# A down product from split operands, and a new order of the arms in an expert loop

## The chip, the cores and the metric

The kernel runs on one core of a Trainium2 chip. The metric is the time of one execution in device microseconds. The core's engines run side by side and meet at semaphores: TensorE (PE in the profile; PEld is its weight load), VectorE (DVE), ScalarE (ACT), GpSimd (POOL) and SyncE (SP). Each has a sequencer that reads its own instruction stream, takes the branches in it and hands the rest to the engine. A row with a q behind the engine (PEldq) is of the sequencer: a branch, a register load or a wait.

## The reference, cut to what matters

Two layers over 1024 latent and 256 context tokens of width 1024. Each ends in a mixture of experts: every token is given to two of 32 experts, and each expert computes

```
def expert_block(args):
    tb, e = args
    xb = h[tb]
    return (jax.nn.silu(xb @ wg[e]) * (xb @ wu[e])) @ wd[e]
```

with `wg`, `wu` of 1024 x 512 and `wd`, the down weights, of 512 x 1024, all float32. The results are scaled by the gates and added up per token. Layer 0 routes all 1280 tokens, layer 1 the 1024 latent ones. How many tokens an expert gets is known only when the router has run.

## The kernel before

After the attention of a layer, `moe` runs the 32 experts one after the other, in straight code with one copy per place `e` in the loop. Experts 0 and 1 always have places 0 and 1 (`FIX`); the others are sorted by size, largest first, when the router is done. `n` is the number of chunks of 64 tokens that the expert at a place has; each engine loads it into a register and branches on it.

The arms differ in `n`. With n=1, `half` multiplies 64 tokens in float32. With n=2, `full` multiplies 128 tokens by gate and up weights together: operands are split into a high and a low part in the type FP32R (`split`: ScalarE copies, VectorE subtracts), and three products of the parts (`mm3`) take the place of one in float32. With n=3 a `full` and a `half` follow each other (`large`). With n=4 `double` computes 256 tokens, and above that `more` takes the rest in pieces. The down product (`down`) is in float32 in every arm: for up to 128 tokens eight matmuls, from four slices `g[:, k]` of the hidden values and two halves of the output.

A place in the loop runs so: first product, then the activation (`act`, ScalarE and VectorE), its transposes (`ht`) mixed with those of the next expert's input (`xt_pe`), the down product, `prep` for the next expert (three of its eight weight slices and its input are split ahead, where its n is over 1), `evac` from PSUM, and the scatter of the rows. The eight weight slices pass through four pairs of buffers, `WS[0]` to `WS[3]`, so slice k uses the pair k % 4. Weights arrive by SyncE's queue in a ring of 14 units, six to an expert, and a unit is loaded again when its last reader is done.

For the order of the code: `with tc.If(...)` lays out the block under it and then the one under `Else`; an engine jumps past the block that it doesn't take. In the first half of the loop (`e < NE // 2`) the long arm stands first:

```
with tc.If(n > 2, preferred_fallthrough_block=True) as c:
    large(e, n, ps, p2, y2, g2)
    nc.tensor.addr_align(256, offset=0, max_nops=0)
with c.Else():
    with tc.If(n > 1, preferred_fallthrough_block=True) as c2:
        full(ps, e)
```

In the second half `half` stands first, then `large`, then `full`. Inside `large` the test L2296 (n < 4) stands ahead of the block for n=3, L2300 (n > 4) ahead of that for n over 4, and the block for n=4 comes last. The lines that the text speaks of: L2345 is the test n > 2 ahead of the first product in the first half of the loop, L2347 the alignment at the long arm's end, L2377 the test n > 2 ahead of the down product; L2115 is the matmul of `half`, L175 to L177 are those of `mm3`, L2082 the transposes of the next input, L2181 the down product, L170 and L171 the two steps of `split`, L2164 VectorE's part of the activation, L2186 and L2187 the evacuation.

Of the kernel before, what the change touches and what calls it, by code (L numbers as in the profile page):

```python
# [10 lines left out]
F32R = mybir.dt.float32r  # L11
# [11 lines left out]
NE = 32  # L23
# [121 lines left out]
class Kernel:  # L145
# [1905 lines left out]
    def moe(self):  # L2051
# [3 lines left out]
        with ExitStack() as ctx:  # L2055
# [8 lines left out]
            self.ring += [wp.tile([128, 2048], F32, name=f"es{i}") for i in range(NU - NU0)]  # L2064
            WS = [(wp.tile([128, 1024], F32R, name=f"wh{i}"), wp.tile([128, 1024], F32R, name=f"wl{i}")) for i in range(NS)]
            G = [sp.tile([128, 4, 128], F32, name=f"g{i}") for i in range(2)]
            SG = [sp.tile([128, 256], F32, name=f"sg{i}") for i in range(2)]
            iv = sp.tile([128, 3], I32, name="iv")
            XT = [sp.tile([128, KD, 128], F32, name=f"xT{i}") for i in range(2)]
# [20 lines left out]
            def xt(x, n):  # L2090
                xt_copy(xt_pe(x), n)
# [16 lines left out]
            def half(ps, e):  # L2108


                x = XT[e % 2]
                for k in range(KD):
                    w = self.unit(e, k // 2)[:, k % 2]
                    for o in range(2):
                        nc.tensor.matmul(ps[0][64 * o:64 * o + 64, :], x[:, k, 0:64], w[:, :, o * 256:(o + 1) * 256],  # L2115
                                         start=(k == 0), stop=(k == KD - 1))
# [8 lines left out]
            def prod(ps, i, k, ns=NS, os=range(2)):  # L2125
                h, lo = [w.rearrange("p (s n) -> p s n", s=2) for w in WS[k % ns]]
                for o in os:
                    c = slice(o * 256, o * 256 + 256)
                    self.mm3(ps[o], XS[i][0][:, k, :], XS[i][1][:, k, :], h[:, :, c], lo[:, :, c],
                             k == 0, k == KD - 1)  # L2130

            def full(ps, e, x=None):

                for k in range(KD - 2):
                    if k + AHEAD < KD:
                        ws(e, k + AHEAD)
                    prod(ps, 0, k)
                for o in range(2):
                    for k in range(KD - 2, KD):
                        prod(ps, 0, k, NS, (o,))  # L2140
                    if x is not None and o == 0:
                        xt(x, e)

            def double(ps, p2, e, m):

# [119 lines left out]
            N = {}  # L2265

            def load_n(e):
                N[e] = nc.values_load(self.seq[0:1, 0, e:e + 1], min_val=0, max_val=2 * nt)
                if e >= FIX:
                    self.E[e] = nc.values_load(self.seq[0:1, 1, e:e + 1], engines=LOADS, min_val=0, max_val=NE - 1)  # L2270

# [21 lines left out]

            def large(e, n, ps, p2, y2, g2):

                with tc.If(n < 4) as c3:  # L2296
                    full(ps, e, xg[2 + e % 3])
                    half(p2, e)
                with c3.Else():
                    with tc.If(n > 4) as c4:  # L2300
                        double(ps, p2, e, 5)
                        hidden(p2, g2)
                        down(g2, e, False)
                        evac(y2)
                        scatter(y2, places(e, 1))
                        more(e, n, 2, p2, g2)
                    with c4.Else():
                        double(ps, p2, e, 4)

            def large_down(e, n, p2, y2, g, g2, pl):  # L2310
                down(g, e, False, (0,))
# [23 lines left out]
            for e in range(NE):  # L2335
                n = N.pop(e)
                nxt = e + 1 if e + 1 < NE else None
                if e + 3 < NE:
                    load_n(e + 3)
                if e + 2 < NE:  # L2340
                    gather(xg[e % 2], first(e + 2, 0, "a"))
                ps, p2, y, y2, g, g2 = GU[e % 2], GU[1 - e % 2], Y[e % 2], Y[1 - e % 2], G[e % 2], G[1 - e % 2]
                if e < NE // 2:

                    with tc.If(n > 2, preferred_fallthrough_block=True) as c:  # L2345
                        large(e, n, ps, p2, y2, g2)
                        nc.tensor.addr_align(256, offset=0, max_nops=0)  # L2347
                    with c.Else():
                        with tc.If(n > 1, preferred_fallthrough_block=True) as c2:
                            full(ps, e)  # L2350
                        with c2.Else():
                            half(ps, e)
                else:
                    with tc.If(n < 2) as c:
                        half(ps, e)
                    with c.Else():
                        with tc.If(n > 2) as c2:
                            large(e, n, ps, p2, y2, g2)
                        with c2.Else():
                            full(ps, e)  # L2360
                self.e_loads(e * 6 + 4 + NU)
                pl = sp.tile([128, 2], I32, name="pl", bufs=4)
                for o, z in enumerate((self.idx_v, self.idx_w)):
                    nc.vector.tensor_copy(pl[:, o:o + 1], z[:, 0, at(e)])
                if e + 3 < NE:
                    over(e + 3)
                s0, s1 = act(ps, 0), act(ps, 1)
                if nxt:
                    x = xt_pe(xg[nxt % 2], (0,))
                ht(ps, s0, g, 0)  # L2370
                if nxt:
                    x += xt_pe(xg[nxt % 2], (1,))
                ht(ps, s1, g, 1)
                if nxt:
                    xt_copy(x, nxt)
                if e < NE // 2:
                    with tc.If(n > 2, preferred_fallthrough_block=True) as c:  # L2377
                        large_down(e, n, p2, y2, g, g2, pl)
                    with c.Else():
                        with tc.If(n > 1, preferred_fallthrough_block=True) as c2:  # L2380
                            down(g, e, False)
                        with c2.Else():
                            down(g, e, True)
                else:
                    with tc.If(n < 2) as c:
                        down(g, e, True)
                    with c.Else():
                        with tc.If(n > 2) as c2:
                            large_down(e, n, p2, y2, g, g2, pl)
                        with c2.Else():  # L2390
                            down(g, e, False)
                if nxt:
                    with tc.If(N[nxt] > 1):
                        prep(nxt)
                evac(y)
                self.e_loads(e * 6 + 6 + NU)
                scatter(y, [pl[:, o:o + 1] for o in range(2)])
                if e >= NE - 3:
                    self.marks.append(nc.gpsimd.memset(self.spacer, 0.0))
                if e == 2:  # L2400
                    self.route_gates()
# [147 lines left out]
```

## Time and profile before

| | |
|---|---|
| Median of three runs | 3205.91 us (3199.2 to 3206.66) |
| The profiled execution | 3205.89 us, of which the span is 3204.1 us |
| TensorE busy | 2653.9 us, 83% of the span |
| VectorE, ScalarE busy | 1507.2 us (47%), 1187.7 us (37%) |
| DMA moved | 617.02 MB, mean 193 GB/s |

The span goes from the first instruction to the last. Busy time counts instructions of the engine itself, not its sequencer's. The expert loop of layer 0 runs from about 868 to 1645 us, that of layer 1 from about 2382 to 3140 us. One float32 matmul gives two records of TensorE, one in FP32R a single record.

### The profile page before, as it was taken

What the parts mean: (1) busy time and instruction counts of PE and PEld (TensorE: products, weight loads), DVE (VectorE), ACT (ScalarE), POOL (GpSimd) and SP (SyncE); (2) the same over time, 40 slices, a digit from 0 to 9 for tenths busy, and PEclk for the clock granted to TensorE, in tenths of its full rate; (3) what the DMA queues carried; (4) which work ended last, traced back from release to release, by engine and by line L of the source; (5) the groups of instructions that cost most, each with busy time, mean ns of one, the idle gap of its engine ahead of it and who ended that gap; (6) DMA issues with size and microseconds to landing.
All of it is one profiled execution on the core that took longest, in us unless ns stands there. A gap on an engine that the chain in (4) does not pass through costs nothing. (4 is left out here: it accounts for less than half of the span.)

```text
span 3204.1 us, 43663 instructions
## 1 busy us (share of the span) xinstructions
PE 2653.9 (83%) x13122; PEld 1670.8 (52%) x13122; DVE 1507.2 (47%) x2981; ACT 1187.7 (37%) x2260; POOL 1064.8 (33%) x919
## 2 busy tenths in 40 slices
PE   6988899998489888987748989999848888887873
PEld 3766556576356445543317765566634455632321
DVE  3355556477644345521149555556852335511115
ACT  3223766632043334511135337665202335511112
POOL 1023999223311121111236349941331111112214
PEclk8988999999699999999978999999969999999987
DMA  7542000042665558899985530002274457799995
GB/s 268 216 139 81 1 1 1 1 157 79 236 245 189 198 181 307 311 351 361 349 315 186 185 136 1 1 1 99 86 260 167 158 196 267 294 363 369 354 357 238
DMA packets 280646, 617.02 MB, mean 193 GB/s; under 512 B 63376, under 2 KB 77072, under 8 KB 271504
## 3 DMA queue, kind: packets, MB, share of 16 engines
q1 hardware_dynamic: 253872, 566.43, 49.0%
q0 software_dynamic: 24544, 37.91, 3.4%
q8 instruction: 281, 4.60, 0.6%
q10 hardware_dynamic: 1536, 4.69, 0.4%
q14 instruction: 413, 3.38, 0.3%
HBM read 577.09 MB, written 73.81 MB: 203 GB/s over the span
## 5 line engine op out<-in xcount | busy, mean ns | idle before, releaser
L2195 POOL DMA_INDIRECT y_d<-my,pl x150 | 166.1, 1107 | 451.2 <-ACT wh L170 194.5
L1330 DVE TENSOR_REDUCE mx<-S 128x1 f32<-128x1024 f32 (+1 forms) x272 | 215.3, 799 | 210.7 <-PE S L1325 210.4
L2181 PE MATMUL mpy<-er,g 128*64 128x512 f32 (+1 forms) x656 | 239.7, 665 | 6.9 <-issue 6.7
L2194 POOL MEMSET spacer<- 128x1 f32 x152 | 17.5, 115 | 665.9 <-DMA y_d<-my,pl 520.5
L175 PE MATMUL gu<-wh,xh 128*128 128x512 f32 x432 | 183.2, 424 | 47.1 <-issue 12.6
L2082 PE MATMUL mtp<-ident,xg 128*128 128x128 f32 x600 | 107.2, 314 | 138.9 <-issue 85.6
L2163 ACT ACTIVATE sg<-gu 128x256 f32<-128x256 f32 x152 | 50.3, 383 | 461.3 <-PE gu L2115 313.9
L1342 ACT ACTIVATE P<-S,nb 128x256 f32<-128x256 f32 (+1 forms) x272 | 208.3, 772 | 33.5 <-DVE nb L1334 32.2
L1356 ACT ACTIVATE PT<-pt 128x512 f32<-128x512 f32 (+1 forms) x321 | 169.1, 531 | 138.2 <-PE pt L1347 129.5
L1347 PE MATMUL pt<-ident,P 128*128 128x128 f32 x1312 | 207.2, 283 | 11.3 <-ACT P L1342 11.1
L2164 DVE TENSOR_TENSOR sg<-gu,sg 128x256 f32<-128x256 f32 x152 | 57.7, 420 | 334.9 <-ACT sg L2163 308.1
L1391 PE MATMUL po<-PT,V 128*64 128x256 f32 x1312 | 215.0, 408 | 0.1
L181 POOL TENSOR_TENSOR rs_out<-ln_ve,mhalf 128x1 f32<-128x1 f32 x64 | 58.7, 917 | 451.0 <-DVE ln_ve L200 292.6
L1347 PEld LDWEIGHTS pt<-ident,P 128*128 128x128 f32 x1312 | 145.2, 141 | 85.5 <-ACT P L1342 42.2
L176 PE MATMUL gu<-wl,xh 128*128 128x512 f32 x432 | 179.5, 416 | 8.9 <-DVE wl L171 8.8
L177 PE MATMUL gu<-wh,xl 128*128 128x512 f32 x432 | 177.4, 411 | 0.0
L2082 PEld LDWEIGHTS mtp<-ident,xg 128*128 128x128 f32 x600 | 82.6, 162 | 178.2 <-issue 167.1
L2115 PE MATMUL gu<-er,xT 128*64 128x512 f32 x704 | 162.2, 607 | 12.3 <-DMA er<-in_w_e_gate 4.8
L1324 PE MATMUL S<-KH,Q 128*128 128x512 f32 (+1 forms) x400 | 168.3, 422 | 1.6 <-ACT P L1342 1.6
L2187 DVE COPY my<-mpy 128x512 f32<-128x512 f32 x75 | 51.7, 690 | 233.9 <-PE mpy L2181 217.6
L171 DVE TENSOR_TENSOR wl<-er,wh 128x1024 fp32r<-128x1024 f32 x106 | 128.1, 1222 | 70.6 <-ACT wh L170 62.7
L1222 POOL TENSOR_TENSOR Y<-Y 128x1310 f32<-128x1310 f32 (+1 forms) x60 | 150.6, 2510 | 5.0
(407 smaller groups left out, 6350.4 us busy)
## 6 DMA issues: line engine op xcount, KB each, us to landing
er<-in_w_e_down SPq DMA_DIRECT2D x66, 1024.0 KB
er<-in_w_e_gate SPq DMA_DIRECT2D x130, 512.0 KB
er<-in_w_e_up SPq DMA_DIRECT2D x130, 512.0 KB
raw<-in_w_mod SPq DMA_DIRECT2D x40, 1024.0 KB
es<-in_w_e_gate SPq DMA_DIRECT2D x68, 512.0 KB
es<-in_w_e_up SPq DMA_DIRECT2D x68, 512.0 KB
es<-in_w_e_down SPq DMA_DIRECT2D x32, 1024.0 KB
raw<-in_w_e_gate SPq DMA_DIRECT2D x40, 512.0 KB
```

The lines of the kernel that those rows point to most:

```text
L175: t.matmul(ps, lh, rh, start=start, stop=False)
L176: t.matmul(ps, lh, rl, start=False, stop=False)
L177: t.matmul(ps, ll, rh, start=False, stop=stop)
L1324: tens.matmul(x[:, c:c + w], q, self.KH[:, g, o:o + w], start=True, stop=False)
L1330: v.tensor_reduce(S[st, "mx"][:, ci:ci + 1], S[st, ci][:, 0:cs[ci][1]], axis=AX.X, op=OP.max)
L1342: act.activation(P[st][:, c:c + w], S[st, ci][:, :w], AF.Exp, bias=S[st, "nb"], accum_out=SU[pi][:, i, h, ci:ci + 1])
L1347: tens.transpose(tp[:, j, :], P[st][:, (g_ * 4 + j) * 128:(g_ * 4 + j + 1) * 128], self.ident)
L1356: act.activation(d, TP[st, g_][:, :m, :], AF.Copy)
L1391: tens.matmul(PO[key][o * 64:o * 64 + 64, :], self.V[:, k0(pi) + j, hp // 2, :], PT[pi, 2 * hp + o][:, j, :], start=(j == 0), stop=(j == n ...
L2082: nc.tensor.transpose(tp[:, j, :], x[:, k * 128:(k + 1) * 128], self.ident)
L2181: nc.tensor.matmul(py[o][64 * o:64 * o + 64, :] if hf else py[o], g[:, k % 2, z:z + 64] if hf else g[:, k, :], self.unit(e, 4 + k // 2)[:, ...
L2195: s = nc.gpsimd.indirect_dma_start(out=self.y_d[0:2 * T, :].rearrange("t (h d) -> (t h) d", h=2), out_offset=bass.IndirectOffsetOnAxis(ap= ...
```

## The change

There is a new down product, `down3`, for n=2. Slice 0 of the hidden values stays in float32. Slices 1 to 3 are split into new tiles `GS`, and the down weights of these slices are split too (`wd`), into the pairs `WS[1]` to `WS[3]`; each then goes through `mm3`. The weights of slice 1 are split near the end of `full` (`dn=True`), those of slices 2 and 3 inside `down3`, when the pairs' last weights of the first product have been read.

In `large` the tests are now n > 3 and, in it, n > 4; the block for n=3 comes last. Experts 0 and 1 take the layout of the second half, with `half` first, and their n is read from `nch` in place of `seq`, the same numbers.

```
@@ def full
-            def full(ps, e, x=None):
+            def full(ps, e, x=None, dn=False):
...
                         ws(e, k + AHEAD)
                     prod(ps, 0, k)
+                if dn:
+                    wd(e, 1)
                 for o in range(2):
                     for k in range(KD - 2, KD):
                         prod(ps, 0, k, NS, (o,))
...
+            def wd(e, k):
+                self.split(*WS[k], self.unit(e, 4 + k // 2)[:, k % 2])
+
+            def down3(g, e):
+                gh, gl = GS
+                for o in range(2):
+                    nc.tensor.matmul(py[o], g[:, 0, :], self.unit(e, 4)[:, 0, o * 512:o * 512 + 512], start=True, stop=False)
+                self.split(gh, gl, g[:, 1:4, :])
+                for k in range(1, 4):
+                    if k > 1:
+                        wd(e, k)
+                    h, lo = WS[k]
+                    for o in range(2):
+                        c = slice(o * 512, o * 512 + 512)
+                        self.mm3(py[o], gh[:, k - 1, :], gl[:, k - 1, :], h[:, c], lo[:, c], False, k == 3)
@@ def load_n
-                N[e] = nc.values_load(self.seq[0:1, 0, e:e + 1], min_val=0, max_val=2 * nt)
+                row = self.nch[0:1, 0, e:e + 1] if e < FIX else self.seq[0:1, 0, e:e + 1]
+                N[e] = nc.values_load(row, min_val=0, max_val=2 * nt)
@@ def large
-                with tc.If(n < 4) as c3:
-                    full(ps, e, xg[2 + e % 3])
-                    half(p2, e)
-                with c3.Else():
-                    with tc.If(n > 4) as c4:
+                with tc.If(n > 3, preferred_fallthrough_block=True) as c3:
+                    with tc.If(n > 4, preferred_fallthrough_block=True) as c4:
                         double(ps, p2, e, 5)
...
                     with c4.Else():
                         double(ps, p2, e, 4)
+                with c3.Else():
+                    full(ps, e, xg[2 + e % 3])
+                    half(p2, e)
@@ the loop over experts, first product
-                if e < NE // 2:
+                if FIX <= e < NE // 2:
...
-                            full(ps, e)
+                            full(ps, e, dn=True)
@@ the loop over experts, down product
-                if e < NE // 2:
+                if FIX <= e < NE // 2:
...
-                            down(g, e, False)
+                            down3(g, e)
```

On TensorE the arm for n=2 of the down product, from its test (L2380 before, L2403 now) to the test ahead of the next expert's first product (L2345 before, L2368 now). `mpy` is the PSUM pair, `er` a ring unit, `g` the hidden values, `gs` their split, `wh` and `wl` the pairs of WS. Before:

```order
L2380 COMPARE_AND_BRANCH
L2181 MATMUL mpy_7378<-er_7087,g_7393 128x512 [waits DMAHW1_49,Activation_49]
L2181 MATMUL mpy_7378<-er_7087,g_7393 128x512
L2181 MATMUL mpy_7378<-er_7088,g_7393 128x512 [waits DMAHW3_49,DMAHW2_49,Activation_49]
L2181 MATMUL mpy_7378<-er_7088,g_7393 128x512
...
L2181 MATMUL mpy_7379<-er_7088,g_7393 128x512 [waits DMAHW4_49]
...
L2345 COMPARE_AND_BRANCH
```

Now:

```order
L2403 COMPARE_AND_BRANCH
L2156 MATMUL mpy_7378<-er_7085,g_7393 128x512 [waits DMAHW5_49,Activation_49]
L2156 MATMUL mpy_7379<-er_7085,g_7393 128x512 [waits DMAHW6_49]
L175 MATMUL mpy_7378<-wh_7386,gs_7394 128x512 [waits Activation_49]
...
L177 MATMUL mpy_7378<-wh_7386,gs_7395 128x512 [waits DVE_49]
...
L175 MATMUL mpy_7378<-wh_7390,gs_7394 128x512 [waits Activation_49]
L176 MATMUL mpy_7378<-wl_7391,gs_7394 128x512 [waits DVE_49]
...
L2368 COMPARE_AND_BRANCH
```

The last wait ahead of the next test was one for a DMA in the seventh of eight matmuls; now it is one for VectorE's low part of slice 3, five records from the end.

On VectorE between the same two places; `xl` is the low part of the next expert's input. Before:

```order
L2380 COMPARE_AND_BRANCH
L2393 COMPARE_AND_BRANCH
L171 TENSOR_TENSOR wl_7385<-er_7089,wh_7384 128x1024 [waits DMAHW4_49,DMAHW3_49,DMAHW5_49,DVE_49,Activation_49]
L171 TENSOR_TENSOR xl<-xT_7397,xh 128x512 [waits Activation_49]
L171 TENSOR_TENSOR wl_7387<-er_7089,wh_7386 128x1024 [waits DVE_49,Activation_49]
```

Now:

```order
L2403 COMPARE_AND_BRANCH
L171 TENSOR_TENSOR gs_7395<-g_7393,gs_7394 128x384 [waits DVE_49,Activation_49]
L171 TENSOR_TENSOR wl_7389<-er_7086,wh_7388 128x1024 [waits DMAHW6_49,DMAHW0_49,DMAHW7_49,DVE_49,Activation_49]
L171 TENSOR_TENSOR wl_7391<-er_7086,wh_7390 128x1024 [waits DVE_49,Activation_49]
...
L2416 COMPARE_AND_BRANCH
L171 TENSOR_TENSOR wl_7385<-er_7087,wh_7384 128x1024 [waits DMAHW1_49,DMAHW0_49,DMAHW7_49,DVE_49,Activation_49]
L171 TENSOR_TENSOR xl<-xT_7399,xh 128x512 [waits Activation_49]
```

Three subtractions stand ahead of `prep`'s five; ScalarE has the three copies for them at the same place.

On TensorE the start of the loop in layer 0, as a piece of the difference; `gu` is the PSUM pair of the first product.

```order
-L2268 TENSOR_LOAD seq
-L2345 COMPARE_AND_BRANCH
-L2296 COMPARE_AND_BRANCH
...
+L2291 TENSOR_LOAD seq
+L2377 COMPARE_AND_BRANCH
+L2116 MATMUL gu_7374<-raw,xT_7399 64x512 x8
...
+L2377 UNCONDITIONAL_BRANCH
+L2380 COMPARE_AND_BRANCH
+L2319 COMPARE_AND_BRANCH
+L2320 COMPARE_AND_BRANCH
```

Behind the first test now stands the half product, and then the tests of the long arm, L2319 (n > 3) and L2320 (n > 4); before, the long arm came behind it.

## Rows read from the trace of the kernel before

**Rows 1.** Page, part 1: the span

```profile
span 3204.1 us, 43663 instructions
```

**Rows 2.** N=2 stretches: span, busy PE PEld DVE ACT POOL, clock, DMA, GB/s

```profile
1172.00:1386.00 214.00, 191.81 (x696) 125.34 (x692) 116.80 (x153) 101.71 (x140) 34.46 (x49) 0.96 0.81 297
...
2652.00:2818.00 166.00, 147.21 (x540) 96.41 (x539) 89.95 (x120) 78.56 (x108) 27.78 (x42) 0.97 0.82 298
```

**Rows 3.** Timeline, ScalarE's evacuations at n=2: start, length, instruction [idle <-releaser]

```profile
1200.66 0.60 ACT L2186 ACTIVATE my<-mpy 128x512 f32<-128x512 f32 x1 [0.85 <-ACT wh L170]
...
1245.82 0.60 ACT L2186 ACTIVATE my<-mpy 128x512 f32<-128x512 f32 x1 [0.86 <-ACT wh L170]
...
1267.35 0.60 ACT L2186 ACTIVATE my<-mpy 128x512 f32<-128x512 f32 x1 [0.84 <-ACT wh L170]
...
1361.00 0.60 ACT L2186 ACTIVATE my<-mpy 128x512 f32<-128x512 f32 x1 [0.84 <-ACT wh L170]
```

**Rows 4.** Timeline of one seam at n=2, all engines

```profile
1238.02 0.76 DVE L2164 TENSOR_TENSOR sg<-gu,sg 128x256 f32<-128x256 f32 x2 [3.59 <-ACT sg L2163]
...
1239.49 1.95 PE L2181 MATMUL mpy<-er,g 128*128 128x512 f32 x4
...
1240.97 1.06 ACT L170 ACTIVATE wh<-es 128x1024 fp32r<-128x1024 f32 x1 [0.47 <-ACTq L2377]
...
1244.72 1.88 PE L2181 MATMUL mpy<-ox,g 128*128 128x512 f32 x4
...
1247.63 0.47 PE L175 MATMUL gu<-wh,xh 128*128 128x512 f32 x1 [1.03 <-DVE my L2187]
...
1247.94 0.40 PE L176 MATMUL gu<-wl,xh 128*128 128x512 f32 x1
...
1248.18 0.40 PE L177 MATMUL gu<-wh,xl 128*128 128x512 f32 x1
```

**Rows 5.** TensorE's sequencer: ns (min/median/max), first and last start

```profile
L2377 PEldq COMPARE_BRANCH  x1: 362/362/362, 1238.8 to 1238.8; - x1
...
L2345 PEldq COMPARE_BRANCH  x1: 6183/6183/6183, 1241.1 to 1241.1; - x1
...
L2345 PEldq COMPARE_BRANCH  x7: 6039/6078/6183, 1196.0 to 1330.8; - x7
...
L2345 PEldq COMPARE_BRANCH  x1: 6687/6687/6687, 868.7 to 868.7; - x1
...
L2345 PEldq COMPARE_BRANCH  x1: 4416/4416/4416, 2650.7 to 2650.7; - x1
```

**Rows 6.** Timeline of TensorE before the first half product of layer 0

```profile
875.92 1.12 PE L2115 MATMUL gu<-raw,xT 128*64 128x512 f32 x2 [7.73 <-ACTq L2349]
```

**Rows 7.** Lines, steps of a split: count, busy us, mean ns, idle

```profile
L170 ACT ACTIVATE wh<-er 128x1024 fp32r<-128x1024 f32 x106 | 111.2, 1055 | 69.0 <-PE gu L177 29.5 <-issue 20.5 <-DVE wl L171 3.3
...
L171 DVE TENSOR_TENSOR wl<-er,wh 128x1024 fp32r<-128x1024 f32 x106 | 128.1, 1222 | 70.6 <-ACT wh L170 62.7
```

**Rows 8.** Stretches around a gap of TensorE, columns as in group 2

```profile
917.00:922.90 5.90, 0.00 (x0) 0.00 (x0) 0.45 (x2) 0.00 (x0) 2.85 (x4) 0.88 1.04 367
...
922.90:928.00 5.10, 5.04 (x16) 4.29 (x17) 0.21 (x1) 1.07 (x2) 0.00 (x0) 0.50 0.79 305
...
928.00:947.00 19.00, 18.24 (x78) 14.44 (x78) 8.08 (x11) 6.09 (x7) 0.67 (x1) 0.99 0.01 3
```

**Rows 9.** TensorE at the end of n=3 (and of n=4, third row)

```profile
1075.49 0.87 PE L2082 MATMUL mtp<-ident,xg 128*128 128x128 f32 x3 [7.40 <-issue]
...
L2347 PEldq COMPARE_BRANCH  x1: 6289/6289/6289, 1068.4 to 1068.4; - x1
...
L2347 PEldq COMPARE_BRANCH  x1: 291/291/291, 945.7 to 945.7; - x1
```

**Rows 10.** Timeline of TensorE in layer 1: first matmuls of places 0 to 3

```profile
2390.38 1.12 PE L2115 MATMUL gu<-raw,xT 128*64 128x512 f32 x2 [7.79 <-ACTq L2349]
...
2410.71 1.98 PE L2115 MATMUL gu<-er,xT 128*64 128x512 f32 x4 [4.77 <-DMA er<-in_w_e_gate]
...
2428.72 0.47 PE L175 MATMUL gu<-wh,xh 128*128 128x512 f32 x1 [2.37 <-ACT my L2186]
...
2523.48 0.76 PE L175 MATMUL gu<-wh,xh 128*128 128x512 f32 x1 [5.76 <-issue]
```

More of the change, by code (lines that the diff above doesn't have):

```diff
@@ L2066, in moe @@
             G = [sp.tile([128, 4, 128], F32, name=f"g{i}") for i in range(2)]
+            GS = [sp.tile([128, 3, 128], F32R, name=f"gs{i}") for i in range(2)]
             SG = [sp.tile([128, 256], F32, name=f"sg{i}") for i in range(2)]
@@ L2359, in moe @@
                         with c2.Else():
-                            full(ps, e)
+                            full(ps, e, dn=True)
                 self.e_loads(e * 6 + 4 + NU)
@@ L2390, in moe @@
                         with c2.Else():
-                            down(g, e, False)
+                            down3(g, e)
                 if nxt:
```

## The prediction

> **What bounds the kernel now.** I read the page's first part, then the stretches of the two expert loops, then TensorE's rows and its sequencer's within single stages. The span is 3204.1 us [rows 1]; the change touches only the two expert loops. The reference's router, run on its inputs, gives how many half chunks n (of 64 tokens) each expert has, and so which arm runs where. Layer 0: expert 0 has n=1, expert 1 n=2, then three with n=4, three with n=3, nine with n=2, fifteen with n=1. Layer 1: experts 0 and 1 n=1, then 7, 4, 4, 3, seven with n=2, nineteen with n=1. So 17 of 64 experts take the new down product, and 16 of them stand in the first half of the loop, where the arm for n>2 comes first in the program.
>
> In the n=2 stretch of layer 0 TensorE is busy 192 of 214 us, and the DMA engines 81% of it [rows 2]. An undisturbed stage there is 21.5 us, from one evacuation at 1245.8 to the next at 1267.4; the seven stages from 1200.7 to 1361.0 take 22.9 us on average [rows 3]. I read the 1.4 us between as late weights.
>
> The reader is to look at the seam between two such stages. The down product, 16 records 0.43 us apart, runs from 1239.49 to about 1246.4, and the next stage's first matmul starts at 1247.63 [rows 4]. What ends last between them is not the copy that the row names, but a branch. TensorE's sequencer reads ahead of its engine: it reaches the test L2345 at 1241.1, when the whole down product is queued, and needs 6.18 us for it, to 1247.3; all seven in this stretch need 6.04 to 6.18 us [rows 5]. With n=2 it jumps past the long arm there. Such a branch does not wait for the engine: the one at 868.7 took 6.69 us [rows 5] while TensorE had nothing to run [rows 6]. I read it as the fetch of the jump's target from memory. At this seam the fetch ends last, not the product.
>
> And the sequencer does not pass a matmul that waits. It reaches L2377 at 1238.8 [rows 5], just as VectorE's second product ends (1238.02 + 0.76 = 1238.78 in [rows 4]), for which the transposes ahead of L2377 wait; before that it had been held there, with the loads for it long queued.
>
> **The down product (17 experts).** Of eight matmuls (16 records of 0.43 us, 6.9 us) two stay (4 records, 1.7 us); 18 single records come, 0.235 us apart as the next stage's at 1247.94 and 1248.18 [rows 4], 4.2 us. TensorE's work falls by 0.95 us, which is worth nothing where the fetch ends later.
>
> What it costs: slices 2 and 3 are split inside the arm, on ScalarE (1.055 us each) and then VectorE (1.222 us each) [rows 7], since their buffers hold the last two weights of the first product. (Slice 1 is split in ScalarE's idle time before that product ends.) On the stage at 1239.5: ScalarE's next split starts at 1240.97 [rows 4]; the split of g takes about 0.5 us (384 of 1024 columns at 1.055 us give 0.4, and a fixed part), to 1241.5; the two weight slices follow to 1242.5 and 1243.5. VectorE subtracts slice 2 from 1242.5 to 1243.75, slice 3 to 1244.95. Only then does the sequencer pass its last wait. Before, it took at most 1.6 us from the product's start at 1239.5 to L2345, with the whole product to queue; with four matmuls left to queue I take 1.15, so 1246.1. With a fetch of 6.1 us and 0.3 us from there to the first matmul (1247.3 to 1247.63) the next stage would start at 1252.5: 4.9 us late, while the product itself ends at 1246.4 as before. The fetch may be shorter, as DMA is less busy in longer stages: 4.4 us was the shortest far jump on this line [rows 5]. I take 5.7 us, so +4.5 us a seam (bounds 3.2 and 5.0). The next expert's splits queue behind the new ones and end near 1250, VectorE's evacuation too, inside that time.
>
> This holds wherever a far jump follows: eight seams in layer 0, seven in layer 1, 15 x 4.5 = +67. (The seam from expert 1 to 2 is below; the last of layer 0 is followed by no far jump.)
>
> The second cost is TensorE's clock. [...] The gap at the seam is 1 us now, 5.5 us then: 15 x 1.7 = +25 (bounds 15 and 37). In return the longer stages hide the late weights: of 15 x 1.4 I take -18 (bounds 0 and -21).
>
> **Chunks first in the long arm.** For n=3 the far jumps now stand at the end: L2347 takes 6.29 us at 1068.4, and TensorE is idle 7.4 us before the transposes at 1075.49 [rows 9]; all four such experts show it, with about 0.8 us of slow clock behind. In the new order the block for n=3 stands last, and its end passes only two short blocks, as the 0.29 us row at 945.7 does after n=4 [rows 9]; but its start gets a jump past the chunk blocks. After an expert with n=4 the long down products hide most of that (+1, twice); after n=3 about 4.5 us show (twice). Sum 4 x -8.2 + 11 = -22. For n=4 one far jump at the start stays one. At its end the jumps pass the n=3 block and the short blocks, 176 and 160 instructions (weight loads counted) instead of 160: between 0 and a fetch less the 4 us of matmuls still queued; I take +2, five times, +10. With n=7 both tests fall through, -2.0 of the 2.37 us idle before 2428.72; the next start has one fetch instead of two, -4.3 of 5.76 us before 2523.48 [rows 10]; the end of n=7 passes more code, +2. In all -22 + 10 - 4.3 = -16.
>
> [...]
>
> **Small arm first for experts 0 and 1.** The half product of expert 0 idles 7.73 us before 875.92 [rows 6] and 7.79 us in layer 1 [rows 10] behind the fetch, though its input is copied within a microsecond. Now it falls through, and the far jump comes behind it, under 8 us of queued matmuls: -6.9 twice. Expert 1 of layer 1 idles 4.77 us before 2410.71 [rows 10]: -4.5. Expert 1 of layer 0 (n=2) keeps its jump; between it and expert 2 the later test (+4.5) meets one fetch instead of two: -0.5. Sum -19. Reading n of experts 0 and 1 from the other tile costs nothing: the same loads.
>
> **Sum** on the profiled run's own time, 3205.89 us (the span and 1.8 us outside it), equal to the median of 3205.91: +67 + 25 - 18 - 16 - 19 = +39, so 3245 us.
>
> **Rivals.**
> A, faster: the next stage does not hang on the later test, because waits of the new matmuls don't hold the sequencer. For it: TensorE's product is 0.95 us shorter. Against: [rows 4, 5]. Then the seams stay where the old fetch ends and the rest remains: -16 - 19 = -35, 3171 us. It decides from where a seam is late by less than 2.3 us in all (35 over 15).
> [...]
> B, no change: the same mechanism with all ends low: 3.2 + 1.0 a seam is 63, less 21, less 35: +7, 3213 us. For it: the row of 4.4 us. Against: seven of seven in the middle of such stages took over 6.0 us.
> C, worse: the chain on ScalarE and VectorE is longer than counted. VectorE's 13 us a stage (116.8 us over nine in [rows 2]) become 17, in one row without a pause, with the next expert's splits and the evacuation behind the new ones. At 1.5 us more a seam it makes +22, 3268 us. For it: the chain has no slack. Against: the fetch covers what follows it.
>
> **Chances.** Forecast 0.62 (its own range 3216 to 3262), A 0.14, B 0.12, C 0.12. A measurement tells about 0.3% here, 9.6 us. Faster is A, 0.14; same is B, 0.12; slower is the forecast and C, 0.74. The range leaves out A and the far end of C: 3192 to 3278 us.
>
> **What would show it.** Right: in n=2 stages the far test is reached about 5 us later after the down product's start, TensorE idles 5 to 6 us before the next first product, the granted clock of this stretch falls below the 0.96 of [rows 2], their stage is 26 to 28 us and their DMA share about 70%; the 7.4 us behind n=3 and the 7.7 us of expert 0 are gone. Wrong: n=2 stages of 21 us or less; the branch reached before the last split ends; or gaps of over 5 us after n=4, by which the arm's new order would cost what it saves.

## The result, and the profile after

The changed kernel takes 3250.1 us at the median of four runs (3237.9 to 3255.9) beside 3202.6 us for the kernel before on the same chip: a ratio of 1.0148, interval [1.0108, 1.0188]. Timed again with more runs (e12 below) it is 1.0176 [1.0157, 1.0196]. So it is slower by about 50 us; the forecast was +39. The sign and the main mechanism came out as forecast. A part of the size came from somewhere else, and several terms of the sum were wrong in ways that cancel in part. The profiled run took 3253.95 us.

First the page of the changed kernel, part 1 (it answers to [rows 1]):

```profile
span 3251.3 us, 44257 instructions
...
PE 2650.2 (82%) x13224; PEld 1701.0 (52%) x13224; DVE 1575.8 (48%) x3049; ACT 1245.2 (38%) x2328; POOL 1080.6 (33%) x919
```

Then the n=2 stretches, cut exactly from the first product of the first such stage to that of the stage behind the last whole one: eight stages in layer 0, seven in layer 1. The columns are those of [rows 2]. Before:

```profile
1178.20:1363.70 185.50, 167.31 (x609) 110.28 (x609) 103.32 (x136) 93.41 (x128) 27.33 (x41) 0.97 0.82 302
2655.40:2817.40 162.00, 145.62 (x532) 95.90 (x532) 86.50 (x114) 76.90 (x106) 24.16 (x38) 0.97 0.81 297
```

After:

```profile
1150.80:1367.80 217.00, 168.76 (x656) 124.60 (x657) 137.89 (x171) 118.98 (x160) 41.48 (x43) 0.88 0.73 264
2661.00:2852.60 191.60, 149.25 (x574) 110.17 (x574) 114.65 (x144) 99.42 (x134) 30.61 (x37) 0.88 0.71 258
```

The reader is to see 31.5 and 29.6 us more for the same 15 stages: 27.1 to 27.4 us a stage instead of 23.2, the clock down from 0.97 to 0.88, and the DMA share down, since the same weights take longer.

One seam of the changed kernel, as a timeline (it answers to [rows 4]): VectorE's split of g and then of the two weight slices, its last split ahead of the next stage, and TensorE's first matmuls of that stage.

```profile
1247.20 0.56 DVE L171 TENSOR_TENSOR gs<-g,gs 128x384 fp32r<-128x384 f32 x1 [0.91 <-ACT gs L170]
...
1248.09 2.36 DVE L171 TENSOR_TENSOR wl<-raw,wh 128x1024 fp32r<-128x1024 f32 x2 [0.33 <-DMA es<-in_w_e_gate]
...
1251.81 0.39 PE L177 MATMUL mpy<-wh,gs 128*128 128x512 f32 x1
...
1255.63 1.22 DVE L171 TENSOR_TENSOR wl<-er,wh 128x1024 fp32r<-128x1024 f32 x1
...
1257.89 0.77 PE L175 MATMUL gu<-wh,xh 128*128 128x512 f32 x1 [5.70 <-issue]
...
1258.45 0.63 PE L176 MATMUL gu<-wl,xh 128*128 128x512 f32 x1
```

And TensorE's sequencer at that seam, then the far test of all eight stages (it answers to [rows 5]; L2403 ends the arm, L2368 is the test that was L2345):

```profile
L2403 PEldq COMPARE_BRANCH  x1: 179/179/179, 1250.5 to 1250.5; - x1
...
L2368 PEldq COMPARE_BRANCH  x1: 6085/6085/6085, 1251.5 to 1251.5; - x1
...
L2368 PEldq COMPARE_BRANCH  x8: 4220/5864/6312, 1146.3 to 1334.2; - x8
```

The product starts at 1245.67. The late splits end at 1248.09 + 2.36 = 1250.45; the branch that closes the arm follows at 1250.51, the far test at 1251.52, 5.85 us behind the product's start, where it was 1.6. It takes 6.08 us, to 1257.60, and the next matmul starts at 1257.89, while the product itself ended at 1252.2. That matmul is 12.2 us behind the product's start, where it was 8.1. The matmuls behind the gap stand 0.43 us apart instead of 0.235, and the stretches around it show why (columns as in [rows 8]):

```profile
1257.90:1261.40 3.50, 3.50 (x8) 2.80 (x9) 0.00 (x0) 0.52 (x1) 1.05 (x1) 0.50 0.92 331
1261.40:1265.00 3.60, 3.60 (x14) 2.87 (x13) 1.92 (x2) 1.97 (x3) 0.00 (x0) 0.82 0.21 80
```

Half of 3.5 us and 0.18 of 3.6 us are lost to the clock, 2.4 us at this seam.

Outside these stretches the two traces differ in two more ways. The stretch of the three n=3 experts of layer 0 (from the first product of one to that of the first n=2 expert) is 111.0 us instead of 129.8. And about 33 us are lost where no product runs: behind the last expert of each layer. There SP's loads for the next part stand late. Before:

```profile
1623.75 0.35 SPq L214 DMA_DIRECT2D g<-mod_d  x1
...
1647.16 1.56 SPq L424 DMA_DIRECT2D yy<-y_d  x3
```

After, with SP's longest wait there (total, times, longest):

```profile
1655.01 0.34 SPq L214 DMA_DIRECT2D g<-mod_d  x1
...
1658.79 2.12 SPq L424 DMA_DIRECT2D yy<-y_d  x3
...
SPq L214 <- DMA y_d<-my,pl: 26.3, 2, 25.0
```

Before, the five loads from g on are issued while the last expert still computes, and only yy waits for the scatters of y_d. After, g itself waits for them, 25.0 us, with all that is queued behind it. The last expert's first product is 2.8 us later than before in layer 0 and 34.7 us in layer 1. Behind them layer 1's first product is 17.9 us later, though the waits ahead of expert 0's product are 5.9 us shorter, and the end of the span 47.2: 21.0 and 12.5 us.

### The profile page after: what moved, and what is told of

Read it like the earlier page. It is cut to its first block, busy times and chain, and to the rows that moved or that the text cites. A ratio compares the mean times of both kernels' runs of the same rounds, so it can differ in the third digit from the quotient of the medians.

```text
span 3251.3 us, 44257 instructions
## 1 busy us (share of the span) xinstructions
PE 2650.2 (82%) x13224; PEld 1701.0 (52%) x13224; DVE 1575.8 (48%) x3049; ACT 1245.2 (38%) x2328; POOL 1080.6 (33%) x919
## 5 line engine op out<-in xcount | busy, mean ns | idle before, releaser
L2217 POOL DMA_INDIRECT y_d<-my,pl x150 | 181.9, 1213 | 489.4 <-ACT my L2208 169.5
L175 PE MATMUL gu<-wh,xh 128*128 128x512 f32 x432 | 192.2, 445 | 102.8 <-issue 63.1
L171 DVE TENSOR_TENSOR wl<-er,wh 128x1024 fp32r<-128x1024 f32 x129 | 156.3, 1223 | 104.6 <-ACT wh L170 76.1
L170 ACT ACTIVATE wh<-er 128x1024 fp32r<-128x1024 f32 x129 | 135.1, 1059 | 124.3 <-PE gu L177 79.0
L2203 PE MATMUL mpy<-er,g 128*64 128x512 f32 (+1 forms) x528 | 176.3, 657 | 0.7 <-issue 0.6
L175 PEld LDWEIGHTS gu<-wh,xh 128*128 128x128 f32 x432 | 90.7, 210 | 135.1 <-issue 112.5
```

What stands on the lines that cost most here:

```text
L175: t.matmul(ps, lh, rh, start=start, stop=False)
L2203: nc.tensor.matmul(py[o][64 * o:64 * o + 64, :] if hf else py[o], g[:, k % 2, z:z + 64] if hf else g[:, k, :], self.unit(e, 4 + k // 2)[:, ...
L2217: s = nc.gpsimd.indirect_dma_start(out=self.y_d[0:2 * T, :].rearrange("t (h d) -> (t h) d", h=2), out_offset=bass.IndirectOffsetOnAxis(ap= ...
```

## The experiments

Each ratio is to the kernel before on the same chip; us are worked out from the ratio with 3200 us.

| run | edit | ratio, interval | us |
|---|---|---|---|
| e12 | changed kernel again | 1.0176 [1.0157, 1.0196] | +56 |
| e1 | gs out of the pool ms | 1.0151 [1.0132, 1.0170] | +48 |
| e2 | before, with gs in ms alone | 1.0040 [1.0025, 1.0055] | +13 |
| e3 | both orders, fp32 product | 0.9902 [0.9878, 0.9927] | -31 |
| e4 | e1, splits run but not read | 0.9955 [0.9939, 0.9972] | -14 |
| e5 | e1, two slices, split early | 1.0012 [0.9995, 1.0029] | +4 |
| e6 | e1, n=2 arm first | 0.9945 [0.9929, 0.9961] | -18 |
| e7, e10 | e3, n=2 arm first | 0.9839 [0.9822, 0.9855], 0.9858 [0.9837, 0.9880] | -52, -45 |
| e8 | before, long arm's order alone | 0.9924 [0.9899, 0.9950] | -24 |
| e9 | e5, n=2 arm first | 0.9988 [0.9973, 1.0003] | -4 |
| e11 | before, small arm first alone | 0.9979 [0.9963, 0.9994] | -7 |

**e1, e2 and e12: the place of the two new tiles.** The theory was that the late loads come from memory, not from late stages. The program's own order says so: SP's load g waits on other queues than before (DMASW are the queues of GpSimd's scatters).

```
before  L214 DMA g_35956<-mod_d 128x1024 [waits DMAHW3_49,PE_49,Pool_49]
after   L214 DMA g_36596<-mod_d 128x1024 [waits DMASW3_49,DMASW4_49,DMASW2_49,DMASW5_49,...]
```

```diff
-GS = [sp.tile([128, 3, 128], F32R, name=f"gs{i}") for i in range(2)]
+GS = [wp.tile([128, 3, 128], F32R, name=f"gs{i}") for i in range(2)]
```

> The changed kernel with its two new tiles gs taken from the weight pool instead of the pool ms, nothing else. In the changed kernel the loads that open the next part (g, ln2g, ln2b, cxt, raw) stand on SP behind a wait of 25 us for the scatters of y_d, at the end of both layers; before, they were issued some 30 us earlier. Theory (place): the 3 KB of gs in ms move the tiles that follow, so that these loads land on a tile that the last scatter still reads. Then the wait goes, and with it about 20 us at the end of layer 0 and 12 us at the end of layer 1: 3250 - 32 = 3218 us. Rival (late stages): the loss at both ends comes from the longer stages, by which the weights arrive otherwise; then 3250 us as the changed kernel.

e2 adds the first of these lines to the kernel before, and nothing else.

> The kernel before with the two tiles gs added in the pool ms; no instruction uses them. Theory (place): the same wait on SP at the end of both layers, 3203 + 32 = 3235 us, all of it behind the last experts. Rival (late stages): no difference, 3203 us.

e1 gave 3248.1 us, e2 3214.2. In e1 the load is back ahead of the last scatter; in e2, which runs the old products, it waits as in the changed kernel:

```profile
1637.83 0.35 SPq L214 DMA_DIRECT2D g<-mod_d  x1
...
1667.31 0.34 SPq L424 DMA_DIRECT2D yy<-y_d  x1
```

```profile
1640.67 0.34 SPq L214 DMA_DIRECT2D g<-mod_d  x1
...
SPq L214 <- DMA y_d<-my,pl: 20.8, 2, 19.5
```

So the wait comes from the tiles' place: that is shown. Its price was missed, 13 us and not 32 in e2, and in e1 nearly nothing came back. To settle this the changed kernel was run again:

> The changed kernel once more, with more runs, to settle what the place of the tiles gs is worth: e2 (gs in ms, nothing else) is 1.004 of before, but e1 (gs moved out of ms) is 1.0151 and the changed kernel was 1.0148 with an interval of 0.004 on both sides. If the place costs in the changed kernel what it costs in e2, this comes out at about 1.0151 + 0.004 = 1.019 (3258 us); if it costs nothing there, at 1.015 (3245 us).

It gave 1.0176, 0.25% or 8 us over e1. By the two intervals this difference alone is within the noise; e2's 13 us (8 to 18) are not. The rest of the 33 us that the two profiles show at the ends of the layers is not explained by the place. A part is only the difference of single executions: from the last expert's first product of layer 0 to layer 1's first it takes 763.8 us before and 778.8 in the profile above, but 768.4 in that of e12, which is the same kernel. And e1's profile, free of the wait, still is late there. The stretch from the last expert's first product to yy takes 27.1 us in e1 and 20.5 before, and 5.24 of the 6.6 us are a gap in which TensorE stands still between two transposes of the last expert and waits for nothing that the profile shows; before, it has no gap at that place.

```profile
1655.25 0.69 PE L2192 MATMUL gu<-ident,sg 128*128 128x128 f32 x2 [5.24 <-issue]
```

Why it stands still is not shown.

**e3 and e4: the product, its splits and the sequencer.** e3 takes the new product away and leaves both orders. e4 runs every split, but the old matmuls, which read none of them.

```diff
 (e4, in down3; the new matmuls go)
 self.split(gh, gl, g[:, 1:4, :])
+wd(e, 2)
+wd(e, 3)
+down(g, e, False)
```

> The changed kernel with the old fp32 down product and without gs; the new order of the long arm and the small arm first stay. From the first products of the two traces the two orders are worth 27 us in layer 0 and 18 us in layer 1: 3203 - 45 = 3158 us, with stages at n=2 of 21 to 23 us as before. By the terms of the prediction (16 + 19) it is 3168 us. If the orders and not the new tiles brought the loss at the ends of the layers, it is 3190 us.

> e1 with the same splits on ScalarE and VectorE, in the same places, but the matmuls of the old fp32 product, which read none of them. Theory (held sequencer): nothing on TensorE waits for the late splits, so the far test is reached 1 to 1.6 us after the product's start and the next stage starts about 1 us behind the product: stages of 21 to 23 us, 3158 us and up to 15 us more where the splits for the next expert come late: 3158 to 3173 us. Rival (length of the ScalarE and VectorE chain, or less matmul work making a worse clock): stages stay at 26 to 28 us and the time at that of e1, about 3218 us.

e3 gave 3164.6 us, e4 3186.6. The eight n=2 stages of layer 0, in e1, e4 and e3:

```profile
1158.70:1377.40 218.70, 167.93 (x657) 124.32 (x657) 136.55 (x168) 117.84 (x159) 31.77 (x42) 0.88 0.72 262
```

```profile
1158.10:1343.90 185.80, 165.68 (x609) 109.37 (x609) 133.94 (x166) 119.25 (x161) 30.59 (x39) 0.97 0.82 302
```

```profile
1148.60:1326.60 178.00, 160.45 (x608) 106.07 (x609) 105.11 (x139) 94.14 (x128) 28.55 (x39) 1.00 0.86 314
```

e4 has the VectorE work of e1 (134 us against 137) and the stages of the kernel before. At a seam of e4 the splits run beside the product just as late, and the far test doesn't wait for them (timeline, then sequencer):

```profile
1243.28 7.11 PE L2197 MATMUL mpy<-raw,g 128*128 128x512 f32 x16
...
1245.70 2.36 DVE L171 TENSOR_TENSOR wl<-raw,wh 128x1024 fp32r<-128x1024 f32 x2 [0.32 <-ACT wh L170]
...
1251.23 0.47 PE L175 MATMUL gu<-wh,xh 128*128 128x512 f32 x1 [0.84 <-ACT my L2202]
```

```profile
L2362 PEldq COMPARE_BRANCH  x1: 5978/5978/5978, 1245.0 to 1245.0; - x1
```

The test is reached 1.7 us behind the product's start, 3.1 us before the last split ends, and the gap is 0.84 us instead of 5.70. So it is the matmuls that wait for the late splits which hold the sequencer. They cost, with the clock, the difference of e1 and e4: 1.96%, 63 us.

e4 less e3 is 17 us, 1.1 us a stage; e4 was expected at 3158 to 3173 us. That is not the work of the splits alone. In five of e4's 15 n=2 stages ScalarE stands still for 3.9 to 4.7 us ahead of its first split for the next product, and waits for nothing that the profile shows; one of them:

```profile
1255.57 1.06 ACT L170 ACTIVATE wh<-er 128x1024 fp32r<-128x1024 f32 x1 [4.59 <-issue]
```

These five stages take 24.7 us on average, the other ten 22.8; in e3, which has no such stop at these places, the 15 take 22.4. So by these single profiles about half of the difference, some 9 us, goes with the stops.

**e5: fewer late waits.**

```diff
 (in full)
-    wd(e, 1)
+    wd(e, 2, 0)      # slice 2 into WS[0]
+    wd(e, 1, 1)      # slice 1 into WS[1]
 (in down3: order of slices 0, 2, 1, 3; 0 and 3 fp32; only g is split there)
```

> e1 with two split slices instead of three, both split before the first product ends (slice 2 into the buffer of weight 4, slice 1 into that of weight 5); slice 3 stays fp32 and comes last. Inside the arm only g is still split (two slices of it). Theory (the sequencer is held until the last late split ends): the last wait moves from the end of slice 3's split (1250.45 in the changed kernel's stage) to the end of g's split (1247.8), 2.7 us earlier, so the next stage starts 2.7 us earlier and the clock loses less: 15 x about 3 us, 3248 - 45 = 3203 us, stages at n=2 of about 24.3 us. Rival (it is the mere sum of split work on ScalarE and VectorE, one slice less of 1.2 us): about 3248 - 15 x 1.2 = 3230 us.

3201.1 us, as the theory has it (3203) and not the rival (3230). Its stretch in layer 0:

```profile
1164.40:1360.50 196.10, 165.44 (x640) 119.27 (x641) 126.35 (x162) 112.07 (x152) 36.06 (x41) 0.94 0.78 287
```

That is 24.5 us a stage, 2.8 less than e1, where the last late wait was moved by 2.7, and the clock is at 0.94.

**e6 and e7: the far jump elsewhere.** The late waits stay in e6, but the n=2 arm is entered without a far jump.

```diff
-with tc.If(n > 2, preferred_fallthrough_block=True) as c:
+with tc.If(n > 2, preferred_fallthrough_block=False) as c:
     large(e, n, ps, p2, y2, g2)
```

> e1 with the arm for n=2 ahead of the arm for n>2 in the program (in the first half of the experts), so that it is entered without a far jump and left with one. Theory: the late splits hold the sequencer as before, but what stands behind them is no far jump, so the next product follows the last one at once (gap 0.3 us instead of 5.7). The far jump starts when the last weight split ends, about 3.2 us before the first product does, and delays the transposes behind it by some 3.2 us. 2.7 us a seam less and a better clock: 3248 - 45 = about 3203 us, with a gap of about 3 us before the transposes. Rival (the gap before the next product comes from splits of the next expert's operands that are late, not from the jump): the gap of 4 us or more stays and the jump's 3.2 us are added, about 3290 us.

> e3 (new orders, old fp32 product) with the arm for n=2 first. Theory: the far jump, hidden under the fp32 product up to 1.0 us in e3, now comes behind the first product, where only 3 us of queued matmuls cover it: the transposes 3.1 us late, the next product 1.0 us early, +2 us a seam and some clock, 3165 + 30 to 40 = 3195 to 3205 us. Rival (a far jump costs the same wherever it stands, or its fetch is hidden): 3150 to 3165 us.

e6 gave 3175.8 us and e7 3145.5, both faster than expected. In e6 the sequencer is held as long as in e1, but what follows takes 67 ns:

```profile
L2403 PEldq COMPARE_BRANCH  x1: 176/176/176, 1250.1 to 1250.1; - x1
...
L2368 PEldq COMPARE_BRANCH  x1: 67/67/67, 1251.1 to 1251.1; - x1
...
L2372 PEldq COMPARE_BRANCH  x1: 5421/5421/5421, 1236.6 to 1236.6; - x1
```

The next product follows without a gap, and e6 is 66 us faster than e1. So most of what the late waits cost comes from the far jump that stands behind them. Not all: e6 is still 28 to 34 us slower than the same order with the old product (e7 and e10). The jump has moved behind the first product (L2372) and delays the transposes there:

```profile
1242.58 1.09 PE L2083 MATMUL mtp<-ident,xg 128*128 128x128 f32 x4 [3.64 <-issue]
```

In e7 that jump hides nearly whole, since it takes 3.4 us and not the 6.1 that the expectation took over from the far test. Sequencer, TensorE's transposes behind it, and the stretch of layer 0:

```profile
L2371 PEldq COMPARE_BRANCH  x1: 3441/3441/3441, 1239.7 to 1239.7; - x1
```

```profile
1243.73 0.52 PE L2082 MATMUL mtp<-ident,xg 128*128 128x128 f32 x3 [0.96 <-DVE sg L2185]
```

```profile
1168.80:1340.40 171.60, 157.96 (x609) 106.27 (x609) 107.48 (x141) 95.57 (x129) 38.39 (x46) 1.00 0.93 340
```

The transposes wait for VectorE now, not for the jump. A stage is 21.45 us on average (seven of the eight take 20.5 to 21.2) with the clock at 1.00 and the DMA engines at 0.93. Run again beside e9 it is still the fastest version:

> e7 once more, on the same chip as e9, for a tight interval and for the comparison with e9: 3145 us, 0.984 of before.

3157.9 us, 0.9858.

**e9: both ideas together.**

> e5 (two split slices, both split early) with the arm for n=2 first, as in e6 and e7. Theory: no far jump stands behind the product and its last late wait ends about 2 us after its start, so TensorE's own work bounds the stage. The product is 8 fp32 records of 0.43 us and 12 single ones of 0.235 us, 6.3 us instead of 6.9: against e7's 21.4 us a stage 0.6 less, 17 x 0.6 = 10 us, so 3145 - 10 = 3135 us, provided that ScalarE and VectorE keep up with three more splits a stage. Rival (these splits delay those of the next product, 1 us a seam as in e4): 3145 - 10 + 17 = 3152 us.

3192.6 us: both expectations missed. The jump behind the first product takes 4.9 us here, as in e6, and starts 2.4 us before that product ends; the transposes come late and take longer (four in 1.09 us, in e7 three in 0.52; at the granted clock of 0.50 behind 1075.49 in the kernel before, three took 0.87 [rows 9]), and the stage is 25.1 us.

```profile
L2372 PEldq COMPARE_BRANCH  x1: 4937/4937/4937, 1261.5 to 1261.5; - x1
```

```profile
1266.95 1.09 PE L2083 MATMUL mtp<-ident,xg 128*128 128x128 f32 x4 [3.14 <-issue]
```

**e8 and e11: the two orders apart.** e8 puts only the new order of the long arm (the edit of large in the change) into the kernel before, e11 only the small arm first with n of experts 0 and 1 from the other tile.

> The kernel before with the long arm's new order alone (chunks first), the old fp32 product and the old order for experts 0 and 1. The prediction's term is -16 (n=3: -22, n=4: +10, n=7: -4): 3182 us. From the places of the first products in e3 and before, three experts with n=3 gain 18 us in layer 0 and the long ones 12 in layer 1, with +4 for n=4: -25, 3173 us.

> The kernel before with the small arm first for experts 0 and 1 alone, and their n read from the other tile. The prediction's term is -19: 3177 us. From e3 (-31) less e8 (-24) it is -7: 3189 us. By the rows, the stretch from the routing's last scatter to expert 0's first product is 5 us shorter in layer 0 and 6 us in layer 1, and a late far jump behind it takes part of that back: -11, 3185 us.

e8 gave 3177.4 us, e11 3189.7. Their -24 and -7 add up to e3's -31.

## Why the prediction was right, and where it was not

**The held sequencer: right.** The prediction put the far test 5.0 us later (1246.1 for 1241.1); it is reached 4.25 us later after the product's start. The fetch, taken as 5.7 us, has a median of 5.86, and the next stage starts 4.1 us late at this seam, forecast 4.5. That it is a fetch is to be seen in the DMA packets of the two traces: in the kernel before each of TensorE's 81 tests of over 2.5 us has a packet of 16 KB of the queue q8, which the page calls instruction, in its time, the last of them ending 1.3 to 2.1 us before the test does; the 423 tests of under 0.5 us have none. In the changed kernel it is 93 of 93, 1.0 to 1.7 us before the end; at this seam the packet goes from 1255.02 to 1256.06 and the test to 1257.60. The reason given for a shorter one, less DMA, holds in part: on L2345 the tests at a DMA share of 0.67 and 0.76 took 4.42 and 5.21 us, the other twenty, at 0.98 and more, 6.04 to 7.11; on L2368 those at 0.69 and 0.72 took 4.22 and 5.23, but the other sixteen, at 0.98 and more, 4.46 to 6.76. e4, e5 and e6 each change one part of this chain (the waits, their time, the jump behind them) and each moves the time the way the chain says. With them rival A is out: the waits do hold the sequencer. B is out by size. C is out too: the chain of the splits ends 4.8 us behind the product's start, where the prediction counted 5.5.

**The terms +67, +25 and -18: right in kind, somewhat too large.** At the seam shown the next stage is 4.1 us late and 2.4 us go to the clock, forecast 4.5 and 1.7. The 1.7 us a gap that make the +25 are shown by no run; what this seam shows in their place are 3.5 us at a granted clock of 0.50 and 3.6 at 0.82. By the stretches above the 15 stages are 61 us longer than before, in e1 64, where 67 + 25 - 18 = 74 was forecast. Against e4 the hold with its clock is worth 63 us, 4 us a seam.

**What was read as late weights** was mostly something else. In five of the 15 n=2 stages of the kernel before ScalarE stands still for 5.4 to 5.7 us ahead of its first split, and waits for nothing that the profile shows. Two of them:

```profile
1206.67 1.06 ACT L170 ACTIVATE wh<-es 128x1024 fp32r<-128x1024 f32 x1 [5.42 <-issue]
...
1341.76 2.95 ACT L170 ACTIVATE wh<-er 128x1024 fp32r<-128x1024 f32 x3 [5.71 <-issue]
```

The stop lies between ScalarE's own test L2345, whose row has 0.05 us, and its next test: 5.4 to 5.7 us in these five stages, 0.4 in the other ten. It may be the fetch of ScalarE's jump, but that is not shown. The five stages take 25.4 us on average, the other ten 22.1. It goes with the layout of the program: e2 and e11, with the old order of the long arm, have it in four and five stages, e3 and e8, with the new one, in none, and their 15 stages take 335.6 and 334.5 us in place of 347.5. In the changed kernel four stages have it, and they are as long as the rest (27.2 and 27.3 us). So the term of -18 was right in that longer stages hide what came late, and wrong in what that was. And in e7 the same weights come in 21.45 us a stage with the DMA share at 0.93, so the 0.81 of [rows 2] was not the rate at which they can come.

**The splits' own work.** The prediction had the next expert's splits and the evacuation "inside that time" and gave them no price. At the seam shown that is so: VectorE's last split ends at 1255.63 + 1.22 = 1256.85, the jump at 1257.60. The 17 us of e4 over e3 show only where nothing is held, and about half of them go with ScalarE's stops. Product in all: 74 forecast, 80 measured over e3 (e1 less e3).

**Chunks first: right in kind, -24 for -16, by other terms.** The 7.4 us behind n=3 are gone, and the entry shows a gap of 3.1 us where 4.5 was taken. The +10 at the end of n=4 (and with it the warning of gaps over 5 us there) is not to be seen in the changed kernel, whose five n=4 experts take 5 us less than before. The sequencer has a longer jump there now, 3.18 us instead of the 0.29 of [rows 9], but it lies under queued matmuls:

```profile
L2370 PEldq COMPARE_BRANCH  x1: 3182/3182/3182, 939.5 to 939.5; - x1
```

```profile
943.60 0.63 PE L2083 MATMUL mtp<-ident,xg 128*128 128x128 f32 x4 [0.38 <-PE gu L177]
```

One packet of 16 KB of q8 moves in these 3.18 us: the row speaks for a fetch that is hidden, not for none.

In e8, which has this order alone, the parts differ again. By its profile the four n=3 experts take 25 us less (forecast -22). The five n=4 experts take 14 us more, not at their end but by gaps inside their first products, such as this one; why is not shown.

```profile
915.82 0.59 PE L175 MATMUL gu<-wh,xh 128*128 128x512 f32 x1 [4.83 <-issue]
```

And the n=2 stages take 13 us less, as ScalarE's stops are gone: for that the prediction has no term.

**The small arm first: the failing step, -7 for -19.** The step said that the far jump "comes behind it, under 8 us of queued matmuls". Expert 0 does start without a wait. But its product of 32 records is not queued whole: the sequencer reaches the jump at 867.8, when 18 records have still to start, and 4.3 us later the product ends (872.1). The jump needs 6.38:

```profile
L2377 PEldq COMPARE_BRANCH  x1: 6380/6380/6380, 867.8 to 867.8; - x1
...
L2416 PEldq COMPARE_BRANCH  x2: 68/1638/3208, 876.6 to 876.7; - x2
...
L2380 PEldq COMPARE_BRANCH  x1: 6764/6764/6764, 880.7 to 880.7; - x1
```

```profile
863.26 5.38 PE L2116 MATMUL gu<-raw,xT 128*64 128x512 f32 x16 [0.87 <-ACTq L2310]
...
868.46 3.62 PE L2116 MATMUL gu<-er,xT 128*64 128x512 f32 x16
874.87 0.63 PE L2083 MATMUL mtp<-ident,xg 128*128 128x128 f32 x4 [2.80 <-issue]
...
887.63 0.76 PE L175 MATMUL gu<-wh,xh 128*128 128x512 f32 x1 [7.67 <-ACT wh L170]
```

The transposes wait 2.80 us for it. Then expert 1 of layer 0, with n=2, reaches its own far jump (L2380) 4.4 us behind the start of expert 0's down product, where before it was 0.9, since a test ahead of it (L2416) takes 3.21 us, where it took 0.2 in the kernel before; the gap ahead of its first product is 7.67 us instead of 3.8. Expert 0's own wait is 0.87 us in place of 7.73, but from its first product to expert 2's it is 51.4 us instead of 47.0, and in e11, which has this change alone, 55.0: in layer 0 nothing of the 6.9 us is left there. The -4.5 for expert 1 of layer 1 failed in the same way. Its 4.77 us (which the row in [rows 10] puts down to a DMA) are gone, but in e11 its transposes now wait 3.09 us, and expert 2's first product 4.63 instead of 2.37:

```profile
2402.60 0.69 PE L2082 MATMUL mtp<-ident,xg 128*128 128x128 f32 x4 [3.09 <-issue]
...
2413.95 0.77 PE L175 MATMUL gu<-wh,xh 128*128 128x512 f32 x1 [4.63 <-DVE cola L2237]
```

**The place of the new tiles: not seen.** The 3 KB of gs in ms were given no step at all. The order of SP in the changed program shows the wait for the scatters, so it could have been seen ahead of the run. It is worth 13 us alone (e2), and some 8 in the changed kernel (e12 less e1, by itself within the noise).

By the runs, then: -31 for the orders, +80 for the product, +8 for the place. These are differences of neighbouring runs, so they add up to e12's +56 by construction; the one check among them is that e8 and e11 give e3. The forecast of +39 had -35 and +74. That it comes so near is in part luck. Counted from the kernel before, as the prediction counts, e1 is +48, of which its n=2 stages are 64 (by the profiles) for the 74; that leaves -16 for everything else, for -35. The two misses, -10 and +19, cancel in part, and the place of the tiles was not in the sum.

## What to carry to other kernels

Here the sequencer's running ahead hid a jump only until the first matmul that had to wait (the far test was reached 5.85 us behind the product's start, for 1.6 before), and only as far as the matmuls queued ahead of it lasted (18 records, 4.3 us, at the place above); so ask, for each far jump, what the last wait ahead of it is and how much is queued behind that. Where a wait can't be had earlier, put the arm that runs most often where it is entered by falling through: here that was worth some 14 to 20 us with the old product and 66 with the new, and the best version of all is the old product with both orders and the n=2 arm first (0.984 to 0.986 of before). And look at the order of the queues after any new tile: two tiles, 3 KB together, made the loads of the next part wait for a scatter, 25.0 us in the changed kernel and 19.5 in e2.

## What the hardware showed that was not expected

The time of a far jump differs by place. The jump into the n=2 arm takes 4.2 to 6.3 us in the changed kernel. The one out of it takes 3.4 us in e7 (eight in a row at most 3.94), yet 5.4 in e6 and 4.9 in e9, where the code between is the same in kind and the down product behind it is longer. What decides it (the place of the target, or the DMA engines' load) no run tells apart; in e9 the longer jump goes with the loss of the whole expected gain. The test L2368, where it falls through in e6, took 0.07 us; the far jumps named here take 50 to 90 times as much.

After the gap of 5.70 us at the seam shown the granted clock was 0.50 for 3.5 us and 0.82 on average for 3.6 more. In e3 and e7, where the gaps between the products of that stretch are 1.5 us or less, its mean was 1.00.
